# One decoder layer on one core: AdaLN's sixth part in the gate-and-up stage, and four smaller moves

## The chip, the cores and the metric

The kernel is one program on one core of a Trainium2 chip (trn2). A core has TensorE for matmuls (PE in the profile, its weight loads PEld), VectorE (DVE), ScalarE (ACT), GpSimd (POOL), and SyncE (SP), which here only issues DMAs. Each engine takes its instructions in program order from its own queue and waits on semaphores for the others. The metric is the time of one execution in microseconds (us), the median of several.

## The reference

A hybrid decoder layer, 1024 tokens wide 1024. AdaLN gives six vectors from the conditioning c; the third (gate_m) and the sixth (gate_f) multiply what the mixer and the feed-forward give.

```python
def reference(x, c, positions, w_ada, b_ada, w_in, sinks, ...):      # x 1 x 1024 x 1024, float32
    c_act = silu(c)
    mod = c_act @ w_ada + b_ada                                      # 6 parts of 1024
    shift_m, scale_m, gate_m, shift_f, scale_f, gate_f = split(mod, 6)
    u = x * (1 + scale_m) + shift_m
    y = mixer(u, ...)          # qkv and two gates from w_in; windowed attention with sinks (16 heads,
                               # 2 kv heads) -> ya; dilated attention (24 heads) -> yb;
                               # (sigmoid(ga) * ya + sigmoid(gb) * yb) @ w_o
    x = layer_norm(ALPHA * x + (1 + gate_m) * y, ln1_g, ln1_b)
    u = x * (1 + scale_f) + shift_f
    y = (silu(u @ w_gate) * (u @ w_up)) @ w_down                     # D_FF = 2816
    return layer_norm(ALPHA * x + (1 + gate_f) * y, ln2_g, ln2_b)
```

## The kernel before

All products are done in two halves of float32: a factor is split into a rounded high part (ScalarE copies it to float32r, `w_hi`) and the rest (VectorE subtracts, `w_lo`), and TensorE does three matmuls hi·hi, hi·lo, lo·hi for each pair of tiles (`mac`). Weights come through the class `Weights` (`ws`): `send` lets SyncE load 128x512 pieces into three buffers `w_raw` ahead of use, `scale` multiplies a piece by a gate on GpSimd where it needs one, `step` splits it. The engines' order is the order of the code (`manual_schedule`): a wait in an engine's queue holds everything behind it.

The stages, in order of time:

1. **Opening.** `c` is loaded and `c_act` = silu(c) worked out on ScalarE and VectorE; `ones` (128x128) is filled by VectorE. `keep_warm(8)` has TensorE multiply `ones` by itself eight times, then two matmuls with `ones` spread `c_act` over all partitions (`pt`, copied to `c_all` by ScalarE), then `keep_warm(21)` fills the time until VectorE has summed the first two AdaLN parts (`ada_sum`), ScalarE has made the first `u`, and the first real matmul (L377) can go.
2. **Projections and attention.** 46 column blocks of w_in, attention for 12 + 8 units, rotary on GpSimd. At the end two gate columns (`tail_gates`) are projected, turned into sigmoids by ScalarE in the tile `r`, and stored to `ga_d`; the last of the two is stored by a DMA from ScalarE's queue.
3. **Border, then gate pairs.** The remaining 12 gate columns are done in pairs by Strassen-Winograd products (`gw`, class `Pairs`): seven products `b11 b21 t2 t1 t3 b22 t4` for eight blocks. The first eight products (n = 0 to 7) use plain weights that `piece()` splits from `w_raw`; their sums of `u` (t2, t1, t3, t4) are read back from DRAM into tiles `xs` (`load_sums`) and split by `next_sums`, one each product. `gw.load` fetches raw weights of a pair, `gw.add` makes their sums on GpSimd.
4. **Branches.** 24 steps (b = 0, 1, 2; dc = 0 to 7), each 24 matmuls and one weight piece; `o_part` splits attention outputs for them. Beside the work of stages 3 and 4 the generator `ada_steps` makes the AdaLN parts 2, 3, 4 and 5: for each part eight row blocks of w_ada (512 KB) are loaded to `a_raw` (two buffers), VectorE adds each, weighted by a value of `c_act`, into `acc` (L993, L995), and TensorE sums `acc` over partitions, by L1008 for the gates (parts 2 and 5) and by L1015 for parts 3 and 4, which go to `shsc`. One call of `next(ada)` is one row block; in steps with b = 0 it is called twice, later once.
5. **w_o.** The merged tiles are multiplied by w_o, whose pieces GpSimd has scaled by gate 2.
6. **Gate and up.** 22 pairs p of columns of w_gate_up, again by seven products (five for p = 0 to 3), `gu.split` made two products ahead (`g_prepare`); GpSimd scales the normalized rows (`gain`) in p = 3 to 10. Results go to DRAM (`h_d`).
7. **w_down and the second layer norm.** w_down's pieces are scaled by gate 5 on GpSimd.

SyncE's DMAs and ScalarE's share eight semaphores in turn; each DMA waits for the one that held its semaphore before.

Of the kernel before, what the change touches and what calls it, by code (L numbers as in the profile page):

```python
# [10 lines left out]
F32 = mybir.dt.float32  # L11
# [7 lines left out]
P = 128  # L19
# [130 lines left out]
def decoder_layer(ctx: ExitStack, tc: tile.TileContext, I, out, dbg=None):  # L150
# [14 lines left out]
    ones = const.tile([P, P], F32, name="ones")  # L165
    nc.vector.memset(ones, 1.0)
# [46 lines left out]
    for x, _ in gate_pairs[:EARLY_PAIRS]:  # L213
        add_chunk(I["w_in"][46 + x], 2, 4)
    for b, dc in steps:
        add_chunk(branch_w[b][dc], 1, 4)
# [15 lines left out]
    ws.limit = len(ws.jobs)  # L232
# [36 lines left out]
    with tc.tile_pool(name="pro", bufs=2) as pro:  # L269
        wa_t, xt_t, raw_t, early_w, mod_t, low_t = {}, {}, {}, {}, {}, {}  # L270
# [532 lines left out]
    def stream():  # L803
# [16 lines left out]
        for dc in tail_gates:  # L820
            g = att.tile([P, T], F32, name="r", bufs=1)
            last = dc == tail_gates[-1]
            sigmoid = act_sigmoid if last else sigmoid_half
            yield from project(46 + dc, lambda t, ps: sigmoid(g[:, t * TH:(t + 1) * TH], ps))
            (nc.scalar if last else nc.sync).dma_start(ga_d[dc], g)
# [155 lines left out]
    ones_r = mix.tile([P, P], F32R, name="ones_r", bufs=1)  # L981
    nc.vector.tensor_copy(ones_r, ones)

    def ada_steps():
        for m in (2, 3, 4, 5):
# [12 lines left out]
            if m in (2, 5):  # L998
                gt = (mix if m == 2 else misc).tile([P, T], F32, name=f"gate{m}", bufs=1)
# [73 lines left out]
    gw.load(0)  # L1073
    load_sums(gp, "xs", 2)
    for step in range(4):
        gw.add(0, step)
# [35 lines left out]
    for n in range(2 * EARLY_PAIRS):  # L1112
# [6 lines left out]
        next_sums(1)  # L1119
        if n == 1:  # L1120
            load_sums(mix, "o_raw", 2)
            gw.load(1)
# [32 lines left out]
    for p in range(len(gate_pairs)):  # L1155
        ps = dict(zip("ab", acc[p])) if p in acc else {}
        g, last = {}, p == len(gate_pairs) - 1
        for i in range(7):
# [16 lines left out]
            if last:  # L1175
                if i == 0:
                    send_parts(2)
                if 2 <= i < 6:
                    parts.append(o_part(bigu))
                if i >= 4:  # L1180
                    ws.step()
            elif p and i in (1, 2, 4, 6) or (p == 1 and i == 3):
                next(ada, None)
# [35 lines left out]
    for i, (b, dc) in enumerate(steps):  # L1219
# [10 lines left out]
        if i == len(steps) - 2:  # L1230
            for x in range(2):
                ws.scale(len(ws.done) + x)
# [10 lines left out]
        for _ in range(2 if b == 0 else 1):  # L1243
            next(ada, None)
# [235 lines left out]

    hs, h_raw = {}, {}
# [10 lines left out]
    for p in range(NF):  # L1492
# [11 lines left out]
        for i in range(7):  # L1504
# [56 lines left out]
            if p == 3 and i == 0:  # L1561
                gb1 = norm_params(1)
            if i == 6 and 3 <= p < 3 + NB:
# [117 lines left out]
```

## Time and profile before

| what | value |
|---|---|
| time, median of 3 runs | 1819.81 us (1819.7 to 1819.91) |
| the profiled execution's own time | 1820.77 us |
| its span, first to last instruction | 1819.0 us |
| PE busy | 1790.4 us (98%) |
| DVE, ACT, POOL busy | 1139.6, 809.9, 621.5 us |
| mean granted TensorE clock | 0.995 |

The page sums each engine's busy time over the span and follows the chain that ended last; the waits view lists who stood still for whom. What stands between 1790.4 us and the span is TensorE's idle time. In the timeline view a row has start (us from the span's start), duration, engine, line, operation, tiles, and in brackets the idle time just before it with what ended it. SPq, ACTq and POOLq are DMA issues.

### The profile page before, as it was taken

How to read it: one execution, taken by the hardware profiler on the slowest of the kernel's cores; microseconds unless marked ns; L12 is line 12 of the kernel's file. 1: busy time of each engine (PE TensorE's matmuls, PEld its weight loads, DVE VectorE, ACT ScalarE, POOL GpSimd, SP SyncE). 2: the span in 40 equal slices, each digit the busy share in tenths (PEclk: the TensorE clock that was granted, in tenths of full speed). 3: DMA queues.
4: the chain of work that ended last, by engine and by line, in shares of the span. 5: the costliest groups of instructions: out<-in, count | busy, mean ns of one | idle time of the engine just before them, and what ended most of it. 6: DMA issues, size and time to landing. Idle time of an engine off the chain costs nothing.

```text
span 1819.0 us, 24567 instructions
## 1 busy us (share of the span) xinstructions
PE 1790.4 (98%) x8906; PEld 1473.9 (81%) x8906; DVE 1139.6 (63%) x2051; ACT 809.9 (45%) x1720; POOL 621.5 (34%) x400
## 2 busy tenths in 40 slices
PE   9999999999999999999979999999999999999998
PEld 7888888888888888878768888888888888888886
DVE  7755566566657766568646965766555444764557
ACT  6654444445444777664522233743333333421122
POOL 0232233233333232125203663156664333532223
PEclk9999999999999999999989999999999999999999
DMA  9322233233233332267466633042222222442222
GB/s 360 96 74 82 83 89 105 85 86 105 83 83 97 84 101 70 83 238 248 158 209 242 208 121 129 12 151 82 81 82 81 94 82 87 151 140 80 92 77 93
DMA packets 93081, 213.83 MB, mean 118 GB/s; under 512 B 15072, under 2 KB 24864, under 8 KB 92960
## 3 DMA queue, kind: packets, MB, share of 16 engines
q1 hardware_dynamic: 92352, 210.61, 35.3%
q8 instruction: 70, 1.15, 0.3%
q0 software_dynamic: 320, 1.06, 0.1%
q10 hardware_dynamic: 288, 0.59, 0.1%
q14 instruction: 51, 0.42, 0.1%
HBM read 163.62 MB, written 34.96 MB: 109 GB/s over the span
## 4 chain that ended last, share of the span: by engine, by line
PE 87%; DVE 5%; DMA 3%; ACT 2%; issue 1%; POOL 1%; SPq 0%; DVEq 0%; POOLq 0%; ACTq 0%
PE pf L1040 23%; PE pj L191 9%; PE pj L193 8%; PE pj L192 8%; PE pf L191 5%; PE pf L192 5%; PE pf L193 5%; PE p L1040 5%; PE s L624 4%; PE po L685 3%; PE pt L662 3%; PE p L191 2%; PE p L193 2%; PE p L192 2%; DMA a_raw<-in_w_ada 1%
## 5 line engine op out<-in xcount | busy, mean ns | idle before, releaser
L191 PE MATMUL pj<-u,w_hi 128*128 128x512 f32 x736 | 302.8, 411 | 0.0
L193 PE MATMUL pj<-u,w_lo 128*128 128x512 f32 x736 | 288.9, 392 | 0.0
L192 PE MATMUL pj<-u,w_hi 128*128 128x512 f32 x736 | 288.3, 392 | 0.0
L551 POOL TENSOR_TENSOR rb<-rb,sin_t 128x512 f32<-128x512 f32 x64 | 85.6, 1338 | 517.0 <-DVE rb L549 466.6
L145 DVE TENSOR_TENSOR w_lo<-r,w_hi 128x512 fp32r<-128x512 f32 x128 | 132.5, 1038 | 137.2 <-ACT w_hi L144 136.7
L191 PEld LDWEIGHTS pj<-u,w_hi 128*128 128x128 f32 x736 | 138.7, 188 | 31.6 <-issue 5.8
L79 DVE TENSOR_TENSOR w_lo<-w_raw,w_hi 128x512 fp32r<-128x512 f32 x132 | 121.0, 920 | 67.9 <-ACT w_hi L78 67.4
L193 PEld LDWEIGHTS pj<-u,w_lo 128*128 128x128 f32 x736 | 138.2, 188 | 30.6
L640 ACT ACTIVATE probs<-probs,st 128x128 f32<-128x128 f32 (+1 forms) x320 | 145.6, 461 | 31.0 <-DVE st L629 30.7
L192 PEld LDWEIGHTS pj<-u,w_hi 128*128 128x128 f32 x736 | 138.9, 189 | 22.3
L192 PE MATMUL pf<-wd,h 128*128 128x512 f32 x352 | 137.1, 389 | 0.0
L193 PE MATMUL pf<-wd,h 128*128 128x512 f32 x352 | 137.1, 389 | 0.0
L191 PE MATMUL pf<-wd,h 128*128 128x512 f32 x352 | 137.1, 389 | 0.0
L62 POOL TENSOR_TENSOR w_raw<-w_raw,gate 128x512 f32<-128x512 f32 x60 | 86.9, 1465 | 144.4 <-DMA w_raw<-in_w_down 117.8
L1594 DVE SCALAR_TENSOR_TENSOR zt<-zt,pf 128x512 f32<-128x512 f32 x112 | 75.2, 684 | 78.9 <-PE pf L193 78.8
L78 ACT ACTIVATE w_hi<-w_raw 128x512 fp32r<-128x512 f32 x132 | 81.7, 622 | 86.9 <-PE p L192 48.8
L552 POOL TENSOR_TENSOR r<-ra,rb 128x512 f32<-128x512 f32 x63 | 116.2, 1845 | 4.9
L664 ACT ACTIVATE ptsb<-pt 128x512 f32<-128x512 f32 (+1 forms) x128 | 63.5, 548 | 99.3 <-PE pt L662 99.0
L565 ACT ACTIVATE qs<-r 64x1024 fp32r<-64x1024 f32 x38 | 40.2, 1059 | 101.4 <-POOL r L552 100.9
L566 DVE TENSOR_TENSOR qs<-r,qs 64x1024 fp32r<-64x1024 f32 x38 | 46.4, 1220 | 57.2 <-ACT qs L565 56.5
L624 PE MATMUL s<-kh,qs 128*128 128x256 f32 (+1 forms) x320 | 79.8, 283 | 2.4 <-DVE st L629 1.7
L624 PE MATMUL s<-kl,qs 128*128 128x256 f32 (+1 forms) x320 | 80.1, 280 | 0.0
(382 smaller groups left out, 4407.5 us busy)
## 6 DMA issues: line engine op xcount, KB each, us to landing
w_raw<-in_w_in SPq DMA_DIRECT2D x100, 256.0 KB
r<-in_w_gate_up SPq DMA_DIRECT2D x44, 512.0 KB
a_raw<-in_w_ada SPq DMA_DIRECT2D x32, 512.0 KB
w_raw<-in_w_down SPq DMA_DIRECT2D x44, 256.0 KB
h_raw<-h_d SPq DMA_DIRECT2D x22, 512.0 KB
h_d<-g SPq DMA_DIRECT2D x39, 256.0 KB
wa<-in_w_ada_m SPq DMA_DIRECT2D x16, 512.0 KB
gt<-ga_d SPq DMA_DIRECT2D x16, 512.0 KB
```

The lines of the kernel that those rows point to most:

```text
L62: self.nc.gpsimd.tensor_tensor(self.raws[i], self.raws[i], scale(), op=OP.mult)
L78: self.nc.scalar.activation(hi, raw, AF.Copy)
L79: self.nc.vector.tensor_tensor(lo, raw, hi, op=OP.subtract)
L145: self.nc.vector.tensor_tensor(lo, src, hi, op=OP.subtract)
L191: nc.tensor.matmul(ps, w[0], m[0], start=first, stop=False)
L192: nc.tensor.matmul(ps, w[0], m[1], start=False, stop=False)
L193: nc.tensor.matmul(ps, w[1], m[0], start=False, stop=last)
L551: eng.tensor_tensor(b, b, sin_t[:, s], op=OP.mult)
L552: eng.tensor_tensor(residue_half(res, r, t), by_residue(a, r), by_residue(b, r), op=OP.add)
L624: nc.tensor.matmul(pss[h][:, i, lo:], box["q"][h][:, b * P:(b + 1) * P], ks[h][:, (b - 1 + lo) * P:(b + 1) * P], start=i == 0 and n == 0, ...
L640: nc.scalar.activation(pr, pr, AF.Exp, scale=-1.0, bias=st[:, 0, h, b:b + 1], accum_out=st[:, 1, h, b:b + 1])
L1040: nc.tensor.matmul(ps, w[:, c], m[:, k], start=first and k == 0 and n == 0, stop=k == 3 and n == 2, skip_group_check=True)
```

## The change

- `ones` is now a float32r tile `ones_r`, seen as float32 through a bitcast; it is filled by a memset of a temporary `one` and a copy, both placed at the start of the pool `pro`, and the later tile `ones_r` of the branch stage goes.
- The last gate of the projection stage uses tile `vt` in place of `r`, and its store is issued by GpSimd.
- At the border, `gw.load(0)` and its sums come after product 0, the loads of the sums two after products 1 and 2 each, `gw.load(1)` after product 4. The first three pieces of w_branch are sent in the last gate pair (`ws.limit`), no longer at the border.
- `ada_steps` makes parts 2, 3 and 4 only, with one call in each branch step. A new generator `last_ada` makes part 5 in the gate-and-up stage: a load after product 3 and an addition after product 6 of each pair from p = 2, then split, bias load, sum on TensorE.
- In the last five branch steps pieces of w_o that are on their way are scaled at once.

```diff
--- before.py
+++ after.py
@@ -162,8 +162,8 @@
     b_pp = const.tile([P, 48], F32, name="b_pp")
     ident = const.tile([P, P], F32, name="ident")
     nc.scalar.dma_start(ident, I["k_ident"])
-    ones = const.tile([P, P], F32, name="ones")
-    nc.vector.memset(ones, 1.0)
+    ones_r = const.tile([P, P], F32R, name="ones")
+    ones = ones_r.bitcast(F32)
 
     def split(hi, lo, src):
         nc.scalar.activation(hi, src, AF.Copy)
@@ -212,6 +212,7 @@
     EARLY_PAIRS = 4
     for x, _ in gate_pairs[:EARLY_PAIRS]:
         add_chunk(I["w_in"][46 + x], 2, 4)
+    ws.limit = len(ws.jobs)
     for b, dc in steps:
         add_chunk(branch_w[b][dc], 1, 4)
     late, wd_t, pools = {}, {}, {"bigu": bigu}
@@ -229,7 +230,7 @@
         for kp in range(4):
             add_chunk(I["w_o"][eh, kp], 2, 1, lambda eh=eh: gates[2][:, eh * 512:(eh + 1) * 512],
                       pair_dest(late, kp, lambda kp: "low", "o_hl") if eh else None)
-    ws.limit = len(ws.jobs)
+    branches_end = len(ws.jobs)
     groups = [2, 3, 4, 3, 3, 3, 4]
     down_pool = lambda f: "low" if sum(f >= e for e in np.cumsum(groups)) % 2 else "bigu"
     for f in range(NF):
@@ -267,6 +268,9 @@
     early_src = [*range(EARLY), 46 + early_gate_dc]
     NE = len(early_src)
     with tc.tile_pool(name="pro", bufs=2) as pro:
+        one = pro.tile([P, P], F32, name="one", bufs=1)
+        nc.vector.memset(one, 1.0)
+        nc.vector.tensor_copy(ones_r, one)
         wa_t, xt_t, raw_t, early_w, mod_t, low_t = {}, {}, {}, {}, {}, {}
 
         def fetch(j):
@@ -818,11 +822,11 @@
                 yield from project(46 + lead_gate_dc, lambda t, ps: act_sigmoid(g[:, t * TH:(t + 1) * TH], ps))
                 nc.sync.dma_start(ga_d[lead_gate_dc], g)
         for dc in tail_gates:
-            g = att.tile([P, T], F32, name="r", bufs=1)
             last = dc == tail_gates[-1]
+            g = att.tile([P, T], F32, name="vt" if last else "r", bufs=1)
             sigmoid = act_sigmoid if last else sigmoid_half
             yield from project(46 + dc, lambda t, ps: sigmoid(g[:, t * TH:(t + 1) * TH], ps))
-            (nc.scalar if last else nc.sync).dma_start(ga_d[dc], g)
+            (nc.gpsimd if last else nc.sync).dma_start(ga_d[dc], g)
 
     lengths = [8 if n == 0 else 24 if "b" in un else 24 if un["a"] == 0 else 8 for n, un in enumerate(units)]
     ends = np.cumsum(lengths)
@@ -978,11 +982,8 @@
 
     shsc = misc.tile([P, 2, KC], F32, name="shsc")
 
-    ones_r = mix.tile([P, P], F32R, name="ones_r", bufs=1)
-    nc.vector.tensor_copy(ones_r, ones)
-
     def ada_steps():
-        for m in (2, 3, 4, 5):
+        for m in (2, 3, 4):
             acc = mix.tile([P, T], F32, name="acc", bufs=1)
             raws = {}
             for k in range(KC + 1):
@@ -995,8 +996,8 @@
                     nc.vector.scalar_tensor_tensor(acc, raws[k - 1], c_act[:, k - 1:k], acc, op0=OP.mult, op1=OP.add)
                 yield
             yield
-            if m in (2, 5):
-                gt = (mix if m == 2 else misc).tile([P, T], F32, name=f"gate{m}", bufs=1)
+            if m == 2:
+                gt = mix.tile([P, T], F32, name="gate2", bufs=1)
                 nc.sync.dma_start(gt, I["b_ada"][:, m * D:(m + 1) * D].to_broadcast([P, D]))
                 hl = [mix.tile([P, T], F32R, name="a_hl", tag="a_raw", bufs=2) for _ in range(2)]
                 split(*hl, acc)
@@ -1070,10 +1071,6 @@
 
     load_sums(mix, "o_raw", 2)
     load_sums(mix, "a_raw", 2)
-    gw.load(0)
-    load_sums(gp, "xs", 2)
-    for step in range(4):
-        gw.add(0, step)
     acc, gated = {}, {}
     done, stored = [], []
 
@@ -1117,8 +1114,15 @@
             piece()
         prepare(n + 4 - 2 * EARLY_PAIRS)
         next_sums(1)
+        if n == 0:
+            gw.load(0)
+            for step in range(4):
+                gw.add(0, step)
         if n == 1:
+            load_sums(gp, "xs", 2)
+        if n == 2:
             load_sums(mix, "o_raw", 2)
+        if n == 4:
             gw.load(1)
         after()
         if n in (4, 6, 7):
@@ -1175,6 +1179,8 @@
             if last:
                 if i == 0:
                     send_parts(2)
+                    ws.limit = branches_end
+                    ws.send()
                 if 2 <= i < 6:
                     parts.append(o_part(bigu))
                 if i >= 4:
@@ -1227,9 +1233,9 @@
             mac(ps[t], w(k), (parts[k][:, 0, s], parts[k][:, 1, s]), k == 0, k == 3)
             if n == 3:
                 ws.step()
-        if i == len(steps) - 2:
-            for x in range(2):
-                ws.scale(len(ws.done) + x)
+        if i >= len(steps) - 5:
+            for j in range(len(ws.done), ws.sent - 1):
+                ws.scale(j)
         if i == len(steps) - 1:
             ws.step()
         if (b == 0 and 2 <= dc < 6) or (b == 1 and dc in (3, 5)):
@@ -1240,8 +1246,7 @@
             parts, following = following, []
         for t in range(2):
             merge(b, dc, t, ps[t], gts.get(i))
-        for _ in range(2 if b == 0 else 1):
-            next(ada, None)
+        next(ada, None)
         fetch_gate(i + 1)
         if i == 2 * KC + 1:
             mg, _ = wide("m", bigu)
@@ -1478,6 +1483,32 @@
             prepared[0] += 1
 
 
+    def last_ada():
+        acc5 = misc.tile([P, T], F32, name="gate5", bufs=1)
+        for k in range(KC):
+            raw = ev.tile([P, T], F32, name="a_raw", bufs=1)
+            nc.sync.dma_start(raw, I["w_ada"][k * P:(k + 1) * P, 5 * D:])
+            yield
+            if k == 0:
+                nc.vector.tensor_scalar(acc5, raw, c_act[:, 0:1], None, op0=OP.mult)
+            else:
+                nc.vector.scalar_tensor_tensor(acc5, raw, c_act[:, k:k + 1], acc5, op0=OP.mult, op1=OP.add)
+            yield
+        hl = [ev.tile([P, T], F32R, name=n, tag=n, bufs=1) for n in ("a_raw", "a_lo")]
+        split(*hl, acc5)
+        yield
+        nc.sync.dma_start(acc5, I["b_ada"][:, 5 * D:].to_broadcast([P, D]))
+        yield
+        for t in range(2):
+            s = slice(t * TH, (t + 1) * TH)
+            ps = ps_x.tile([P, TH], F32, name="px")
+            for x in range(2):
+                nc.tensor.matmul(ps, ones_r, hl[x][:, s], start=x == 0, stop=x == 1)
+            nc.vector.tensor_tensor(acc5[:, s], ps, acc5[:, s], op=OP.add)
+        nc.vector.tensor_scalar(acc5, acc5, 1.0, None, op0=OP.add)
+        gates[5] = acc5
+
+    ada = last_ada()
     hs, h_raw = {}, {}
 
     def h_load(f):
@@ -1560,6 +1591,8 @@
                     ws.step()
             if p == 3 and i == 0:
                 gb1 = norm_params(1)
+            if p > 1 and i in (3, 6):
+                next(ada, None)
             if i == 6 and 3 <= p < 3 + NB:
                 gain(p - 3, gb1)
     gb2 = norm_params(2)
```

The order of instructions shows three places. First VectorE's queue at the very start (`ones`, `one`: the 128x128 tiles of ones; `wa`: AdaLN weights). Before:

```order
L166 MEMSET ones 128x128
L175 TENSOR_SCALAR c_act<-c_act 128x8
L176 RECIPROCAL c_act<-c_act 128x8
L177 TENSOR_TENSOR c_act<-c_act,c_raw 128x8
L309 TENSOR_TENSOR diag<-ident,c_act 128x512 x2
L328 TENSOR_SCALAR b_pp<-b_pp 128x8
```

Now:

```order
L175 TENSOR_SCALAR c_act<-c_act 128x8
L176 RECIPROCAL c_act<-c_act 128x8
L177 TENSOR_TENSOR c_act<-c_act,c_raw 128x8
L272 MEMSET one 128x128
L273 CAST ones<-one 128x128
L313 TENSOR_TENSOR diag<-ident,c_act 128x512 x2
```

The filling of `ones` has moved behind the three instructions on `c_act`, and a copy has been added.

Second, SyncE's queue at the border between projection and gate pairs. Before:

```order
L55 DMA w_raw<-in_w_in 128x512
L728 DMA wb<-wa_d 64x1024 x2
L1058 DMA xs<-t_d 128x2x512 x4
L112 DMA r_7655<-in_w_in 128x1024
L112 DMA r_7656<-in_w_in 128x1024
L1058 DMA xs<-t_d 128x2x512 x2
L55 DMA w_raw<-in_w_in 128x512 x3
L1058 DMA xs<-t_d 128x2x512 x2
L112 DMA r_7721<-in_w_in 128x1024
L112 DMA r_7722<-in_w_in 128x1024
L55 DMA w_raw<-in_w_branch_a 128x512 x3
```

Now:

```order
L55 DMA w_raw<-in_w_in 128x512
L732 DMA wb<-wa_d 64x1024 x2
L1059 DMA xs<-t_d 128x2x512 x4
L55 DMA w_raw<-in_w_in 128x512 x2
L112 DMA r_7682<-in_w_in 128x1024
L112 DMA r_7683<-in_w_in 128x1024
L55 DMA w_raw<-in_w_in 128x512
L1059 DMA xs<-t_d 128x2x512 x4
L112 DMA r_7778<-in_w_in 128x1024
L112 DMA r_7779<-in_w_in 128x1024
```

Two of the weight pieces have moved ahead of the raw weights of the first pair, the third ahead of the sums of t3 and t4; the branch pieces are no longer here.

Third, VectorE's queue in the gate-and-up stage, from product 6 of one pair to product 1 of the next (`g`: the two halves of h; `c`: a kept product; `s`: the sums whose splits are the weights of t2 and t1). Before:

```order
L145 TENSOR_TENSOR w_lo<-r_11123,w_hi 128x512
L1536 TENSOR_TENSOR g<-g,pf 128x512
L1537 TENSOR_TENSOR g<-g,c_11264 128x512
L145 TENSOR_TENSOR w_lo<-s_11225,w_hi 128x512
L145 TENSOR_TENSOR w_lo<-s_11224,w_hi 128x512
L1530 TENSOR_TENSOR g<-g,pf 128x512
```

Now:

```order
L1567 TENSOR_TENSOR g<-g,pf 128x512
L1568 TENSOR_TENSOR g<-g,c_11233 128x512
L1495 SCALAR_TENSOR_TENSOR gate_10956<-a_raw,c_act,gate_10956 128x1024
L145 TENSOR_TENSOR w_lo<-s_11192,w_hi 128x512
L145 TENSOR_TENSOR w_lo<-s_11191,w_hi 128x512
L1561 TENSOR_TENSOR g<-g,pf 128x512
```

One addition of 128x1024 stands between the second product of the gate (L1568) and the split for t2.

## The prediction

> **What bounds the kernel now.** The page comes first: it says which engine has no room.
>
> ```profile
> PE 1790.4 (98%) x8906; PEld 1473.9 (81%) x8906; DVE 1139.6 (63%) x2051; ACT 809.9 (45%) x1720; POOL 621.5 (34%) x400
> ```
>
> TensorE is the bound. The change adds no matmul and takes none away, so it can gain at most what TensorE idles or runs slowly, and it loses wherever a new wait reaches TensorE. The waits view lists who keeps TensorE (total us, times, longest):
>
> ```profile
> PE p L1015 <- DVE acc L995: 11.2, 1, 11.2
> PE p L1040 <- DVE w_lo L79: 2.9, 2, 2.0
> PE p L1008 <- DVE a_hl L170: 1.4, 1, 1.4
> PE po L317 <- DVE ones L166: 1.1, 1, 1.1
> PE p L191 <- DVE gy L1208: 1.0, 1, 1.0
> PE pj L363 <- ACT u L348: 0.3, 1, 0.3
> ```
>
> Four of the six are touched: L1015 (part 3 of AdaLN), L1040 (the border), L191 (w_o), and L317 (the opening). The table of stages then shows where there is no idle time to hide anything in:
>
> ```profile
> 1200.00:1400.00 200.00, 200.00 (x884) 165.65 (x884) 115.38 (x116) 78.23 (x140) 120.21 (x72) 1.00 0.27 92
> ```
>
> In gate and up TensorE is busy 200 of 200 us; VectorE (115) has room on average, but only the moment counts.
>
> **The long wait goes.** The timeline of TensorE around it, and around its twin for part 4 (the same eight small matmuls without a wait):
>
> ```profile
> 928.00 0.39 PE L193 MATMUL p<-o_hl,w_lo 128*128 128x512 f32 x1
> 939.60 3.54 PE L1015 MATMUL p<-ones,acc 128*128 128x1 f32 x16 [11.21 <-DVE acc L995]
> 943.00 0.78 PE L191 MATMUL p<-o_hl,w_hi 128*128 128x512 f32 x1
> ...
> 946.02 0.39 PE L192 MATMUL p<-o_hl,w_hi 128*128 128x512 f32 x1
> ...
> 976.87 0.39 PE L193 MATMUL p<-o_hl,w_lo 128*128 128x512 f32 x1
> ...
> 978.90 0.48 PE L191 MATMUL p<-o_hl,w_hi 128*128 128x512 f32 x1
> ...
> 980.59 0.39 PE L192 MATMUL p<-o_hl,w_hi 128*128 128x512 f32 x1
> ```
>
> From the last ordinary matmul to the first one after L1015 it is 15.00 us (928.00 to 943.00) against 2.03 for the twin (976.87 to 978.90): 12.97 lost. Then the clock is still down: the next seven starts take 3.02 us (to 946.02) against 1.69 (978.90 to 980.59), 1.33 more. Together **14.3 us**, more than the 11.2 of the waits view. Why `acc` is late:
>
> ```profile
> 913.04 1.32 SPq L991 DMA_DIRECT2D a_raw<-in_w_ada  x2
> 922.51 1.28 DVE L995 SCALAR_TENSOR_TENSOR acc<-a_raw,c_act,acc 128x1024 f32<-128x1024 f32 x1 [10.55 <-DMA a_raw<-in_w_ada]
> ```
>
> Each branch step with b = 0 asks for two row blocks (1 MB) beside its weights, and a block issued at 913.04 is there at 922.5, 9.5 us later. The step lasts 5.44 us (24 matmuls, 0.227 apart). With one call per step, the matmul of part 3 moves from the end of step 3 (928.2) to the end of step 7, 928.2 + 4 x 5.44 = 950.0. Even if each of the blocks 3 to 7 took 9.5 us and two were in flight, the chain from 913.0 goes 922.5, 924.4, 933.5, 935, 944.3 and the last addition ends at 945.6: 4.4 us in hand. Taken: the whole 14.3; bounds 0 and 14.3. VectorE stands still on blocks meanwhile, but a step's weight piece is split before its addition and needed three steps later, so TensorE does not feel it. Part 4 follows at the end of step 17 and is used only after w_o.
>
> **The border.** The waits of 2.05 and 0.90 us:
>
> ```profile
> 799.21 0.50 PE L1040 MATMUL p<-u,w_lo 128*128 128x512 f32 x1 [2.05 <-DVE w_lo L79]
> 799.55 0.63 PE L1040 MATMUL p<-u,w_hi 128*128 128x512 f32 x2
> 785.59 9.49 SPq L1058 DMA_DIRECT2D xs<-t_d  x2
> SPq L1058 <- DMA ga_d<-r: 8.7, 1, 8.7
> 794.71 1.06 ACT L1029 ACTIVATE t2h<-xs 128x1024 fp32r<-128x1024 f32 x1 [6.39 <-DMA ga_d<-r]
> 800.25 0.63 ACT L78 ACTIVATE w_hi<-w_raw 128x512 fp32r<-128x512 f32 x1 [3.01 <-DMA w_raw<-in_w_in]
> ```
>
> One store is behind both: `ga_d<-r`, issued by ScalarE. ScalarE's copy to t2h waits 6.39 us for it (with the next weight split queued behind), and SyncE's next load waits 8.7 us for it because the store holds the semaphore whose turn it is; the three weight pieces queued behind it are issued only after 795.1 (785.59 + 9.49). With the store on GpSimd's queue and from `vt`, SyncE's turn and t2h are free of it, and two pieces go out ahead of the first pair's weights. Each wait also costs 0.11 for the refill (0.34 from 799.21 to 799.55, otherwise 0.23). Gain **3.2 us**, bounds 0 and 3.2. Late next, at worst: the raw weights of pair 0, now issued only when the second piece's buffer is free, and needed as sums at the ninth product, eight products of 12 matmuls (2.7 us each) after the first.
>
> **w_o.** TensorE waits 0.96 for a bank that `gy` frees:
>
> ```profile
> 1056.07 0.39 PE L191 MATMUL p<-w_hi,m 128*128 128x512 f32 x1
> 1053.04 0.63 ACT L78 ACTIVATE w_hi<-w_raw 128x512 fp32r<-128x512 f32 x1 [5.51 <-POOL w_raw L62]
> 1058.23 2.38 DVE L79 TENSOR_TENSOR w_lo<-w_raw,w_hi 128x512 fp32r<-128x512 f32 x2
> 1060.54 1.27 DVE L1208 TENSOR_TENSOR gy<-p,gt 128x512 f32<-128x512 f32 x2
> ```
>
> The last branch step, whose banks `gy` empties, ended where w_o begins, at 1056.07; VectorE came 4 us late, held by two splits of pieces that GpSimd had scaled late. Scaled sooner, and with part 5 gone from VectorE here, `gy` comes 2 to 3 us sooner. Gain **1.1 us** (0.96 and a refill), bounds 0 and 1.1. The 1.4 of L1008 (part 2) stays: its order is unchanged.
>
> **The opening, a cost.** TensorE's first work waits for `ones`:
>
> ```profile
> 0.84 0.17 DVE L166 MEMSET ones<- 128x128 f32 x1 [0.84 <-PEq L1670]
> 3.54 0.17 DVE L177 TENSOR_TENSOR c_act<-c_act,c_raw 128x8 f32<-128x8 f32 x1
> 786.57 0.21 DVE L982 CAST ones_r<-ones 128x128 fp32r<-128x128 f32 x1
> 4.63 3.18 PE L321 MATMUL pt<-diag,ones 128*128 128x512 f32 x4
> 7.65 4.85 PE L317 MATMUL po<-ones 128*128 128x128 f32 x42
> 10.89 0.63 ACT L348 ACTIVATE u<-ut 128x512 fp32r<-128x512 f32 x1
> 18.44 1.02 PE L363 MATMUL pj<-u,e_hi 128*128 128x512 f32 x2 [0.34 <-ACT u L348]
> ```
>
> `ones` was ready at 1.01. In the new order the memset stands behind L177, which ends at 3.71 because it waits for `c`; with memset and copy (0.17 and 0.21) `ones` is ready at 4.09: 3.1 us later. TensorE then runs eight warming products, L321, 21 more, and the first real matmul at 12.25 without a gap, while `u` was ready at 11.52. All of that, `u` included (it hangs on L321), moves by 3.1. Only the wait of 0.34 at 18.44, set by a load, swallows some. After it TensorE has no idle time until the attention, so **+2.8 us** stays; bounds 0 (the loads set the pace) and 3.1.
>
> The rows above show the rate full again at 946.02, 6.4 us after work resumed at 939.60. [...]
>
> **Gate and up, a cost.** An addition of 128x1024 now stands in front of the split for t2:
>
> ```profile
> 1305.87 2.75 POOL L1366 TENSOR_TENSOR zt<-zt,gb 128x1024 f32<-128x1024 f32 x1
> 1306.87 2.31 DVE L1537 TENSOR_TENSOR g<-g,c 128x512 f32<-128x512 f32 x1
> 1309.10 1.28 DVE L145 TENSOR_TENSOR w_lo<-s,w_hi 128x512 fp32r<-128x512 f32 x2
> 1310.90 0.39 PE L1040 MATMUL pf<-t2h,w_lo 128*128 128x512 f32 x1
> 1381.97 0.68 DVE L1537 TENSOR_TENSOR g<-g,c 128x512 f32<-128x512 f32 x1
> L995 DVE SCALAR_TENSOR_TENSOR acc<-a_raw,c_act,acc x28: 1272/1284/2312, 833.0 to 1026.5; 128x1024 f32<-128x1024 f32 x28
> ```
>
> The split for t2 ends at 1309.78 and its weight load starts 0.23 before 1310.90, at 1310.67: 0.9 us in hand. The addition takes 1.28 (median), so the split ends at about 1310.98. By the border's rows the matmul starts 0.05 after, the next 0.34 later, at 1311.37 in place of 1311.13: 0.24 us lost. This place comes once a pair; eight additions are made (p = 2 to 9), but p = 2's feeds a pair without the first two products and is a short first one. So 7 x 0.24 = **1.7 us**. Bounds: 0 if VectorE comes earlier, and 8.9 if each addition takes the longest of the 28, 2.31 (1.03 more, 7 x 1.27). Taken near the low end: the GpSimd work that doubles L1537 (2.31 against 0.68 without it) ends at 1308.62, before the addition starts. The rest of part 5 costs nothing: its four matmuls (0.9) leave the branch stage and come back here, the splits for p = 10 and the last sums on VectorE have 2 us and more in hand, and each load has a whole pair (19 us) to land.
>
> **The sum.** -14.3 - 3.2 - 1.1 + 2.8 + 1.7 = -14.1. The profiled execution took 1820.77 (span 1819.0 and 1.77 around it): span 1804.9, time 1806.7. The median of the runs is 0.96 below that execution, so the forecast for the median is **1805.7 us**.
>
> **Rivals.** (1) *The new costs are hidden* (0.15): the opening is paced by loads and the split for t2 slips through: -18.6, 1801.2. The 0.34 at 18.44 speaks for it, the gapless TensorE from 12.25 on against. (2) *The additions run into GpSimd* (0.13): 8.9 in place of 1.7, 1812.9. It needs GpSimd's gain 0.5 us later than it is. [...] (3) *The long wait only moves* (0.05): a block takes over 10.5 us to land and TensorE waits at step 7 as it did at step 3: 14.3 back, 1820.0, no change. The widest landing seen, 9.5, speaks against it. (4) *The border still waits*, now for the store on GpSimd's queue or the later raw weights (0.05): 1808.9. (5) *Slower* (0.04): in gate and up a row block lands after VectorE wants it. VectorE then holds the split for t2 and TensorE stands, eight times. A block's buffer is free when the addition before it ends (1310.4 in the rows above), and the next addition comes a pair later (84 matmuls, 19.0 us, after 1309.1): 17.7 us. At 21 us of landing 3.3 are lost eight times, 26 us, and the time is 1832; past the 1823.4 of a measurable loss it gets at 19.9 us. Against it: this stage's DMA share of 0.27 at 92 GB/s, to which the blocks add 27.
>
> **How the numbers follow.** The forecast holds 0.58. A measurement of this kernel tells 0.2% (3.6 us) from no change: 1816.2 and below is faster. Forecast and rivals 1, 2 and 4 are (0.91); rival 3 is no change (0.05); rival 5 slower (0.04). The range 1801.5 to 1811.5 takes the forecast with the bounds of the opening, the border and w_o, most of rival 1, and rival 2 up to additions of about 2.1 us.
>
> **What would show it.** Right: no L1015 wait in the waits view and a granted clock of 1.00 from 900 to 950; no L1040 wait at the border; TensorE's first matmul at about 4.2 and the first real one at about 15.4; seven short waits of TensorE for `w_lo` in gate and up, 0.1 to 0.3 each. Wrong: a wait on `acc` or `a_raw` at step 7, a first real matmul at 12.3, or waits over 1 us in gate and up.

## The result

The changed kernel takes **1805.86 us** (median of six, 1804.71 to 1806.85) against 1819.69 us (median of six, 1817.68 to 1819.91) of the kernel before on the same chip: ratio 0.9926, 95% interval 0.9913 to 0.9939, or 13.8 us less. The forecast was 1805.7. The profiled execution took 1804.71 us with a span of 1802.9.

### The profile after

The first line of the page's first part (busy time, share and instructions of each engine), then the waits view of TensorE (total us, times, longest):

```profile
PE 1786.3 (99%) x8906; PEld 1469.5 (82%) x8906; DVE 1147.7 (64%) x2051; ACT 810.3 (45%) x1720; POOL 619.2 (34%) x401
```

```profile
PE po L321 <- DVE ones L273: 4.1, 1, 4.1
PE s L628 <- DVE st L633: 1.7, 6, 0.3
PE p L1009 <- DVE a_hl L170: 1.4, 1, 1.4
PE pf L191 <- DVE zt L1325: 0.9, 1, 0.9
PE pf L1041 <- DVE spare L1450: 0.3, 1, 0.3
```

The 11.2 for `acc`, the 2.9 for `w_lo` at the border and the 1.0 for `gy` are gone. The wait for `ones` is longer, as expected; that for `zt` (0.26 before) and the one for `spare` were not in the forecast. The 1.4 for `a_hl` stays. The seven waits in gate and up do not show here, since the weight load waits in TensorE's place; they stand in the waits view of the weight loads and, for one pair, in the timelines of VectorE and of the weight loads:

```profile
PEld pf L1041 <- DVE w_lo L145: 2.7, 7, 0.4
```

```profile
1291.21 1.27 DVE L1495 SCALAR_TENSOR_TENSOR gate<-a_raw,c_act,gate 128x1024 f32<-128x1024 f32 x1
1292.41 1.28 DVE L145 TENSOR_TENSOR w_lo<-s,w_hi 128x512 fp32r<-128x512 f32 x2
1293.14 0.19 PEld L1041 LDWEIGHTS pf<-t2h,w_lo 128*128 128x128 f32 x1 [0.38 <-DVE w_lo L145]
```

The addition ends, the split starts, and the weight load comes 0.38 after it was due. The place of the long wait now, in TensorE's timeline and in the table of stages (busy time of PE, PEld, DVE, ACT, POOL with counts, granted clock, DMA share, GB/s):

```profile
946.54 0.39 PE L193 MATMUL p<-o_hl,w_lo 128*128 128x512 f32 x1
946.77 1.84 PE L1016 MATMUL p<-ones,acc 128*128 128x1 f32 x16
948.47 0.49 PE L191 MATMUL p<-o_hl,w_hi 128*128 128x512 f32 x1
```

```profile
900.00:950.00 50.00, 50.00 (x231) 41.66 (x230) 24.99 (x30) 22.14 (x36) 0.03 (x1) 1.00 0.70 228
```

Part 3 is summed at 946.77 without a wait and TensorE is busy for all 50 us at clock 1.00. The last addition into `acc` stands on VectorE like this, so 9.3 us were in hand (937.43 to 946.77):

```profile
936.15 1.28 DVE L996 SCALAR_TENSOR_TENSOR acc<-a_raw,c_act,acc 128x1024 f32<-128x1024 f32 x1
```

The opening, TensorE:

```profile
4.12 3.46 PE L321 MATMUL po<-ones 128*128 128x128 f32 x16 [4.12 <-DVE ones L273]
7.41 1.88 PE L325 MATMUL pt<-diag,ones 128*128 128x512 f32 x4
9.13 4.85 PE L321 MATMUL po<-ones 128*128 128x128 f32 x42
13.74 0.48 PE L381 MATMUL pj<-u,e_hi 128*128 128x512 f32 x1
```

TensorE starts 3.06 later than before, but its first real matmul (L381) comes only 1.49 later: the four matmuls on `diag` took 1.88 in place of 3.18. The trace's own record of the clock explains it: the rate rose from half to full at 7.09, 3.0 us after TensorE's start, so all four ran fast; before, it rose at 7.21, 6.2 us after the start, and three of the four ran slowly.

### Where the time went

The same matmul looked up in both timelines, at the ends of the stages. The last column is the step from one row to the next.

| matmul | before | after | difference | step |
|---|---|---|---|---|
| first real one | 12.25 | 13.74 | +1.49 | +1.49 |
| behind the load wait of the opening | 19.29 | 20.40 | +1.11 | -0.38 |
| end of the attention | 779.08 | 779.62 | +0.54 | -0.57 |
| end of the plain products, after the border | 889.69 | 886.48 | -3.21 | -3.75 |
| first of w_o | 1056.07 | 1037.50 | -18.57 | -15.36 |
| w_o, behind the place of `gy` | 1061.27 | 1041.58 | -19.69 | -1.12 |
| second half of w_o | 1101.27 | 1082.04 | -19.23 | +0.46 |
| opening of gate and up | 1171.59 | 1152.67 | -18.92 | +0.31 |
| t2 of the pair after the last addition | 1349.21 | 1332.08 | -17.13 | +1.79 |
| t3, after part 5's matmuls | 1373.01 | 1356.85 | -16.16 | +0.97 |
| last matmul | 1810.70 | 1794.57 | -16.13 | +0.03 |

The step of -15.36 holds the four matmuls of part 5, which come back later as the +0.97; the long wait alone is 14.39. The total, 16.1, is larger than the 13.8 between the medians: the profiled execution of before (1820.77) was slower than its median and had the longest ramp of the clock seen in the opening, that of the change was the fastest of its six and had the shortest. The two ramps differ by 1.57 (12.25 - 1.06 = 11.19 against 13.74 - 4.12 = 9.62), which is no effect of the change, as the runs below show.

### The profile page after: what moved, and what is told of

It is laid out like the page before. It is cut to its first block, busy times and chain, and to the rows that moved or that the text cites. A ratio compares the mean times of both kernels' runs of the same rounds, so it can differ in the third digit from the quotient of the medians.

```text
span 1802.9 us, 24555 instructions
## 1 busy us (share of the span) xinstructions
PE 1786.3 (99%) x8906; PEld 1469.5 (82%) x8906; DVE 1147.7 (64%) x2051; ACT 810.3 (45%) x1720; POOL 619.2 (34%) x401
## 4 chain that ended last, share of the span: by engine, by line
PE 94%; DVE 3%; ACT 2%; issue 1%; POOL 0%; DMA 0%; DVEq 0%; ACTq 0%
PE pf L1041 23%; PE pj L191 9%; PE pj L193 9%; PE pj L192 8%; PE p L1041 6%; PE pf L191 5%; PE pf L193 5%; PE pf L192 5%; PE s L628 4%; PE p L191 3%; PE p L193 3%; PE p L192 3%; PE po L689 3%; PE pt L666 3%; DVE qs L570 1%; ACT probs L644 1%
## 5 line engine op out<-in xcount | busy, mean ns | idle before, releaser
L145 DVE TENSOR_TENSOR w_lo<-r,w_hi 128x512 fp32r<-128x512 f32 x128 | 140.2, 1099 | 118.7 <-ACT w_hi L144 118.3
L79 DVE TENSOR_TENSOR w_lo<-w_raw,w_hi 128x512 fp32r<-128x512 f32 x132 | 124.8, 949 | 81.3 <-ACT w_hi L78 80.8
L126 POOL TENSOR_TENSOR s<-r 128x512 f32<-128x512 f32 x27 | 36.1, 1336 | 128.1 <-DVE w_lo L145 96.4
```

The costliest lines, as they stand in the source:

```text
L79: self.nc.vector.tensor_tensor(lo, raw, hi, op=OP.subtract)
L145: self.nc.vector.tensor_tensor(lo, src, hi, op=OP.subtract)
```

## The experiments

All edits are on the changed kernel. "Control" is the changed kernel itself, run again beside the runs that move the ones and the additions and beside the first faster version. The runs with two calls, with halves of the border undone and with the scaling undone were made on another chip; a later series of the changed kernel there (the second control below) gave 1805.52 in place of 1806.70, so a difference of about 1 us between the medians of these runs and the control proves nothing, and the timelines decide.

### The changed kernel again, and the opening

> The changed kernel again, unaltered, as the measure for the runs beside it. Two readings of the result stand against each other. (a) The sum of the prediction was right as it stands (-14.1): this execution again lies 13 to 15 us below the kernel before in the median, and its opening may show a ramp of the clock of another length than the 3.3 us that the first profile showed (the kernel before: 6.1), because the ramp varies from one execution to the next. (b) The short ramp belongs to the later start: the profile shows 3.3 us of half rate again, within 0.3, and the first real matmul again at 13.7 within 0.3.

Measured: **1806.70** (1806.06 to 1807.5), ratio to before 0.9925 (0.9912 to 0.9939). From first matmul (3.92) to first real one (14.49) it took 10.57, not 9.62; the clock rose 4.9 us after the first matmul, not 3.0. Reading (a) holds: the short ramp was chance.

Now the tile of ones is filled first again:

```diff
+    with tc.tile_pool(name="first", bufs=1) as first:
+        one = first.tile([P, P], F32, name="one")
+        nc.vector.memset(one, 1.0)
+        nc.vector.tensor_copy(ones_r, one)
     c_act = const.tile([P, KC], F32, name="c_act")
...
-        one = pro.tile([P, P], F32, name="one", bufs=1)
-        nc.vector.memset(one, 1.0)
-        nc.vector.tensor_copy(ones_r, one)
```

> The tile of ones is filled at the head of VectorE's queue again, the rest as changed. The prediction's term (+2.8, the opening shifts everything) expects 2.8 us less than the control, first matmul at about 1.3, first real one 2.8 or more before the control's. The rival, that later waits swallow the shift (the wait of 0.34 for u at 18.4 and that of 0.6 for qs in the attention, which come back here), expects 0.4 to 1.1 us less than the control. A third, that the opening is set by loads altogether, expects no difference, within 0.3.

Measured: **1804.89** (1804.49 to 1805.36), 1.8 below the control; ratio to before 0.9915 (0.9902 to 0.9929). TensorE's timeline and two rows of the waits view:

```profile
1.32 3.78 PE L323 MATMUL po<-ones 128*128 128x128 f32 x16 [1.32 <-DVE ones L176]
...
11.94 0.48 PE L383 MATMUL pj<-u,e_hi 128*128 128x512 f32 x1
...
18.32 1.02 PE L369 MATMUL pj<-u,e_hi 128*128 128x512 f32 x2 [0.54 <-ACT u L354]
```

```profile
PE s L630 <- DVE qs L572: 0.6, 1, 0.6
```

The ramp was the control's (10.62 against 10.57), so the two timelines can be compared: the first real matmul comes 2.55 earlier, 1.98 are left behind the wait for `u`, 1.6 at the end of the attention, 1.9 at 900 and 2.2 at the end of the program. The opening passes on some 2 us, between the prediction's 2.8 and the 0.4 to 1.1 of the rival reading. What swallows the rest is as the rival said, the waits for `u` (0.54) and `qs` (0.6 against 0.2).

### One call or two per branch step

```diff
-        next(ada, None)
+        for _ in range(2 if b == 0 else 1):
+            next(ada, None)
```

> Branch steps with b = 0 ask for two row blocks again, as before; the rest as changed. The prediction's account of the long wait (the matmul of part 3 stands at the end of step 3 while the blocks land 9.5 us after their issue) expects the wait of TensorE for acc back, 10 to 12 us, with the clock at half rate for some 3 us after it: 14.3 us above the control of 1806.7, about 1821. The rival, that the wait belonged to the crowd of loads at that time, which part six, the border loads and the pieces sent sooner have changed, expects a much smaller wait, 0 to 6 us, and 1807 to 1813.

Measured: **1820.89** (1817.87 to 1827.45, nine), 14.2 above the control (15.4 above the second one, on the same chip) and no faster than before (ratio 1.001, 0.9998 to 1.0023). Waits view and TensorE's timeline:

```profile
PE p L1016 <- DVE acc L996: 8.9, 1, 8.9
PE pf L191 <- DVE zt L1326: 1.8, 1, 1.8
```

```profile
925.88 0.39 PE L193 MATMUL p<-o_hl,w_lo 128*128 128x512 f32 x1
935.13 3.54 PE L1016 MATMUL p<-ones,acc 128*128 128x1 f32 x16 [8.85 <-DVE acc L996]
938.53 0.77 PE L191 MATMUL p<-o_hl,w_hi 128*128 128x512 f32 x1
```

One line brings the long wait back with its half rate (0.77 for the next matmul), although part 5 is out of the branch stage and the border is as changed. The number of calls is the cause. That moving part 5 is what allows one call is argued, not tried: part 4 came ten steps behind part 3 (1003.02 and 946.77), and a third part would end behind the last of the 24 steps. In the profiled execution the loss in the branch steps is 12.4, and 1.0 more is the wait for `zt`; the wait itself is 2.4 shorter than before, so the crowd of loads had a small share. The spread of its nine times is about 10 us. The two longest had the lowest granted clock (1827.45 at 0.992, 1824.52 at 0.993, the shortest 1817.87 at 0.995), so part of the spread is time at half rate; the rest is open.

### The border, undone by halves

The store back on ScalarE's queue and in tile `r`, the new order of loads kept:

```diff
-            g = att.tile([P, T], F32, name="vt" if last else "r", bufs=1)
+            g = att.tile([P, T], F32, name="r", bufs=1)
...
-            (nc.gpsimd if last else nc.sync).dma_start(ga_d[dc], g)
+            (nc.scalar if last else nc.sync).dma_start(ga_d[dc], g)
```

> The last gate is stored by ScalarE from the tile r again; the new order of the border loads stays. If the store is behind both border waits, as predicted, ScalarE's copy to t2h waits 5 us or more for it again, and a load of SyncE's waits 5 us or more for its semaphore; TensorE waits for w_lo 1 to 3 us at the border: 1 to 3.2 us above the control of 1806.7. If it was the order of the loads that took the waits away, TensorE waits 0.3 or less there and the time is the control's within 0.3.

Measured: **1808.43** (1806.78 to 1809.23), 1.7 above the control (2.9 above the second); ratio to before 0.9937 (0.9922 to 0.9952). ScalarE's timeline, SyncE's waits and TensorE's waits:

```profile
795.68 1.06 ACT L1030 ACTIVATE t2h<-xs 128x1024 fp32r<-128x1024 f32 x1 [5.37 <-DMA ga_d<-r]
```

```profile
SPq L112 <- DMA ga_d<-r: 2.9, 1, 2.9
```

```profile
PE p L1041 <- ACT sx L1145: 1.3, 1, 1.3
PE p L1041 <- DVE w_lo L145: 0.6, 2, 0.4
PE p L1041 <- ACT gt L1142: 0.2, 1, 0.2
```

The store holds ScalarE 5.37 again, but no plain product waits: the pieces ahead in SyncE's queue were there. ScalarE and VectorE fall behind by the splits of the sums, and TensorE pays 15 us later, at 810 to 820, for `w_lo` of the first pairs, `gt` and `sx`. From the end of the attention to 890 the execution loses 2.8 against the control's.

The old order, with the store as changed:

```diff
     load_sums(mix, "a_raw", 2)
+    gw.load(0)
+    load_sums(gp, "xs", 2)
+    for step in range(4):
+        gw.add(0, step)
...
-        if n == 0:
-            gw.load(0)
-            for step in range(4):
-                gw.add(0, step)
         if n == 1:
-            load_sums(gp, "xs", 2)
-        if n == 2:
             load_sums(mix, "o_raw", 2)
-        if n == 4:
             gw.load(1)
...
-    ws.limit = len(ws.jobs)
     for b, dc in steps:
         add_chunk(branch_w[b][dc], 1, 4)
...
-    branches_end = len(ws.jobs)
+    ws.limit = len(ws.jobs)
...
-                    ws.limit = branches_end
-                    ws.send()
```

> The border loads go out in the old order again (the raw weights of the first pair ahead of the plain pieces, the branch pieces at the border); the store stays on GpSimd's queue and in the tile vt. If the store alone was behind the waits, the border has no wait over 0.5 and the time is the control's 1806.7 within 0.5. If the order carries them, TensorE waits 2 to 3 us for w_lo at the border: about 1809.5.

Measured: **1807.97** (1807.33 to 1809.52), 1.3 above the control (2.5 above the second); ratio 0.9937 (0.9922 to 0.9952). TensorE's waits and ScalarE's timeline:

```profile
PE p L1040 <- ACT w_hi L78: 0.8, 1, 0.8
```

```profile
801.34 0.63 ACT L78 ACTIVATE w_hi<-w_raw 128x512 fp32r<-128x512 f32 x1 [9.36 <-DMA w_raw<-in_w_in]
```

The store is out of the way (the copies to t2h wait for nothing), yet the pieces queued behind 1 MB of raw weights and two sums land late by themselves: 9.36 us of ScalarE, 0.84 of TensorE. From the end of the attention to 890 this execution loses 1.2 against the control's. The halves, 2.8 and 1.2, come to 4.0; the whole step was 3.75 in the two timelines above, and 3.2 in those of both controls.

### Scaling sooner, undone

```diff
-        if i >= len(steps) - 5:
-            for j in range(len(ws.done), ws.sent - 1):
-                ws.scale(j)
+        if i == len(steps) - 2:
+            for x in range(2):
+                ws.scale(len(ws.done) + x)
```

> Pieces of w_o are scaled in the last step but one again, two of them, as before; the rest as changed. The prediction's term for w_o expects the wait for gy of about 1.0 back and 1.1 us more than the control of 1806.7. The rival, that taking part 5 from VectorE's queue there was enough, expects no such wait and the control's time within 0.3.

Measured: **1806.03** (1805.36 to 1806.38), 0.7 below the control, 0.5 above the second, and so within the spread of such runs; ratio 0.9925 (0.991 to 0.9939). The view of TensorE's waits has no row for `gy`; the longest row of the second half of the program is

```profile
PE pf L191 <- DVE zt L1325: 1.1, 1, 1.1
```

So scaling sooner gains nothing on its own. What took the wait away is then, by the rows, part 5's leaving VectorE's queue: in the kernel before, its last two instructions (L1009, L1010) hold VectorE from 1042.02 to 1044.60, ahead of the last three `gy`, and the last starts 4.5 us behind the first matmul of w_o; here it starts 2.5 behind, with the sooner scaling 1.5. No run puts part 5 back alone.

### The additions in another place

```diff
-            if p > 1 and i in (3, 6):
+            if (p > 1 and i == 5) or (p > 2 and i == 4):
                 next(ada, None)
```

> The additions of part 5 are made after product 4 of each pair from p = 3 on, in front of a split that has 2 us in hand, and the loads after product 5; the rest as changed. The prediction's term for gate and up (7 x 0.24 = 1.7) expects the seven waits of the weight loads for w_lo (0.38 each) to be gone and the time 1.7 to 1.8 us below the control. The rival, that an addition anywhere in VectorE's queue costs TensorE as much (it only moves), expects waits of the same size at another product and no difference, within 0.3.

Measured: **1805.68** (1805.43 to 1807.12), 1.0 below the control; ratio 0.9922 (0.991 to 0.9935). The row of seven waits is gone from the weight loads, and one new wait stands in TensorE's timeline:

```profile
1348.81 0.50 PE L1041 MATMUL pf<-b21h,w_lo 128*128 128x512 f32 x1 [1.40 <-DVE w_lo L145]
```

Up to 1334 the timelines show 0.25 to 0.3 gained at each pair, the prediction's price; then the split of part 5 (128x1024, on ScalarE and VectorE), which this edit moved too, to after product 5 of pair 10, takes 1.4 and a refill back. By the timelines the edit nets 0.3; the rest of the 1.0 is a shorter ramp in the opening. The rival, that an addition costs as much anywhere, falls.

### Towards a faster version

The first had ones first, the additions moved as above, one more `yield` between the split of part 2 and its matmul, and two PSUM tiles allocated and not used ahead of w_o's eight:

```diff
                 split(*hl, acc)
                 yield
+                yield
...
+    for _ in range(2):
+        ps_2.tile([P, TH], F32, name="p2")
     banks = [ps_2.tile([P, TH], F32, name="p2") for _ in range(NB)]
```

> Ones first, additions after product 4, one more step between the split of part 2 and its matmul (the wait of 1.4 for a_hl, with its refill 1.5), and two PSUM banks of w_o passed over in turn, so that the first product of the second half of w_o gets the bank that it had before (wait for zt 0.26 in place of 0.85). By the prediction's terms: -2.8 - 1.8 - 1.5 - 0.6 = 6.7 us below the control; if later waits swallow the opening, 4.3 to 5.0 below it. Against that stands that a wait taken away comes back at the next place, as a wait for another tile: then 2 us or less below the control.

Measured: **1803.21** (1802.56 to 1805.73), 3.5 below the control; ratio 0.9909 (0.9895 to 0.9922). The wait for `a_hl` is gone and the 1.40 above is there; the wait for `zt` has grown to 1.56. The unused tiles moved nothing. VectorE's timelines show what the wait hangs on. The additions that empty the eight PSUM banks of w_o's first half (`zt`) run in the order of the row blocks 0 to 7, and the waiting matmul starts 0.15 us behind the end of one of them: of block 4 in the kernel before, of block 5 in the changed one, and of block 6 in this one and in the one with two calls. That is the block whose bank the second half takes first. The matmul that waits, in the kernel before, the changed one, this one and the one with two calls:

```profile
1101.27 0.47 PE L191 MATMUL pf<-o_hl,m 128*128 128x512 f32 x1 [0.26 <-DVE zt L1320]
```

```profile
1082.04 0.47 PE L191 MATMUL pf<-o_hl,m 128*128 128x512 f32 x1 [0.85 <-DVE zt L1325]
```

```profile
1080.37 0.47 PE L196 MATMUL pf<-o_hl,m 128*128 128x512 f32 x1 [1.56 <-DVE zt L1328]
```

```profile
1096.51 0.47 PE L191 MATMUL pf<-o_hl,m 128*128 128x512 f32 x1 [1.82 <-DVE zt L1326]
```

Next, part 5's split went to product 3 of pair 11 and two of w_o's tiles were exchanged:

```diff
+            if (2 <= p <= 9 and i == 5) or (3 <= p <= 10 and i == 4) or (p, i) in ((11, 3), (11, 5), (12, 3)):
                 next(ada, None)
...
+    banks[3], banks[6] = banks[6], banks[3]
```

> The changed kernel once more, for the run beside it: 1806.7 within 0.7; from TensorE's first matmul to its first real one 9.6 to 11.2 us, the spread that nine executions of these kernels have shown.

> Ones first; additions after product 4, the split of part 5 after product 3 of pair 11 in place of product 5 of pair 10; one more step between the split of part 2 and its matmul; and two banks of w_o exchanged, so that the bank that the second half of w_o takes first (bank 0) is that of the fourth row block, not of a late one. By the waits seen: opening -1.8, additions -1.8, a_hl -1.5, zt -0.9: 6.0 us below the control, about 1800.7, with no wait for zt and none of 1.4 for w_lo in gate and up. If the bank of the second half of w_o is not what sets the wait for zt, that wait stays at 0.8 to 1.6 and the time is 1801.6 or more.

Measured: control **1805.52** (1805.13 to 1806.14), lower than was expected, this **1801.96** (1801.65 to 1803.03), 3.6 less; ratio to before 0.9908 (0.9894 to 0.9923). The 1.4 for `w_lo` is gone, but `zt` waits 2.07. The exchange in the code did not help: the matmul still starts 0.15 behind the addition of block 6. So the expectation on `zt` missed through its edit, not through the mechanism. The last edit leaves the banks and changes the order in which VectorE empties them:

```diff
+    turn = [0, 1, 2, 3, 6, 4, 5, 7]
-    for tb in range(NB):
-        residual(banks[tb], tb, 0)
+    for n, tb in enumerate(turn):
+        residual(banks[tb], tb, 0)
```

(with x loaded in the same order, and without the exchange).

> As the best so far (ones first, additions after product 4, one more step for part 2), and in w_o the block whose bank the second half takes first is added and released ahead of the other three late ones (the order of the blocks on VectorE is 0 1 2 3 6 4 5 7). If the bank sets the wait for zt (before: bank of block 4, wait 0.26; changed: block 5, 0.85; later variants: block 6, 1.6 to 2.1), the wait falls to 0.5 or less and the time to 1800 to 1800.8. If the loads of x are late for any order, the wait stays above 1 and the time at 1802.

> The same without the new order of blocks, for comparison on the same chip: 1802.0 within 0.7, wait for zt 1.5 to 2.2.

Measured: **1800.42** (1799.99 to 1800.75), ratio to before **0.9891** (0.9878 to 0.9905), against 1803.15 (1801.31 to 1804.29), ratio 0.9905 (0.9892 to 0.9918), of the version without the new order on the same chip (its median is above the 1802.0 within 0.7 that was expected, its `zt` waits 1.5). The wait:

```profile
1079.86 0.47 PE L196 MATMUL pf<-o_hl,m 128*128 128x512 f32 x1 [0.19 <-DVE zt L1328]
```

The matmul again starts 0.15 behind the addition of block 6, which is now the fifth. So the bank sets this wait; of the 2.7 between the two medians it accounts for 1.3. This version beats both kernels: 19.3 us below the one before on the same chip, some 5 below the changed one as its three series showed it (1805.86, 1806.70, 1805.52).

## Why the prediction was right, and where it was not

The mechanism, the direction and the total are right, and the long wait, 14.3 of the 14.1 net, was the term that mattered. By its terms:

| term | predicted | in the two timelines | by experiment |
|---|---|---|---|
| long wait of part 3 | -14.3 | -14.39 | two calls: +14.2 |
| border | -3.2 | -3.75 (both controls -3.2) | halves: 2.8 and 1.2 by timeline, 1.7 and 1.3 by medians |
| w_o | -1.1 | -1.12 | not from the scaling |
| opening | +2.8 | +0.54, with equal ramps about +2.1 | ones first: -1.8 |
| gate and up | +1.7 | +1.79 | seven waits gone when moved |
| not foreseen | - | zt +0.46, spare +0.31 | zt: the bank |
| sum | -14.1 | -16.1, with equal ramps -14.6 | medians: -13.8 |

**The long wait.** The step count was exact: part 3 came at 946.77, and 950.0 less the 3.2 already gained is 946.8. The blocks came sooner than the bound that was worked out, so 9.3 us were in hand, and rival 3 (the wait only moves) never came near.

**Gate and up.** Price and count held: 0.26 a pair, seven times. Rival 2 did not come: the seven additions took 1.27 each, each behind the GpSimd instruction beside which L1568 took 2.30 (L1371; 0.68 at 1365.84, with no GpSimd work beside it) and which ended 0.47 us before the addition began, as the rows of before had said. Rival 5 did not come either: no addition of this stage waited for its row block.

**The border** was rightly sized and wrongly explained. "One store is behind both" failed: with the store undone alone the two waits on plain pieces stayed away, and with the order undone alone one of them came back. The store's cost is the lag of ScalarE and VectorE, the order's the lag of the pieces; in the kernel before both fell on the same matmuls and looked like one.

**w_o.** The size was right, and of the two reasons that the prediction gave together (scaled sooner, part 5 gone from VectorE) the second is enough: the wait stayed away with the scaling undone. `gy` came 2.0 sooner without the sooner scaling and 3.0 with it, as the prediction had it.

**The opening** was mis-sized: 2.8 against about 2. The step that failed rests on "After it TensorE has no idle time until the attention": that holds, but in the attention TensorE waits for `qs` (0.6 before and with ones first, 0.2 in the control), and that wait shrank, as did the one for `u` (0.34 before, none after). A delay is not passed on whole through a later wait on something that does not move with it: with ones first the gain of 2.55 was 1.98 behind the wait for `u`. That the two timelines show only 0.54 is the ramp: it was 1.57 shorter, which is also why the first real matmul came at 13.74 and not at the forecast 15.4. The prediction's sum took the ramp as in the kernel before (11.19). In the profiled execution it was shorter by 1.57; in the control, with the same late start, by 0.62. Three executions of the changed kernel took 9.62, 10.57 and 9.72 from the first matmul to the first real one: it differs from one execution to the next, and leaving it out of the sum for the median was right.

**Not foreseen.** The bank that the second half of w_o takes first is that of row block 5 in place of 4: 0.46. Which of the edits moved it was not tried; the run with two calls, where part 5 is gone too, had block 6. And in the opening of gate and up a split for `spare` (0.31) that was just in time came late; with ones first this wait is absent, and its cause was not traced.

So the closeness of 1805.7 to 1805.86 owes something to luck: in the two timelines 0.7 too much for the opening and 0.5 too little gained at the border stand against 0.8 of waits left out, and the medians moved 0.8 less than the timelines with equal ramps.

## What to carry to other kernels

When a generator is advanced once or twice per step, work out from the trace how long one of its loads takes to land and at which step its last consumer stands: here the step back to two calls, one line, took the whole gain away. In gate and up an addition of 1.27 us cost 0.26 a pair ahead of a split with 0.9 us in hand, and its seven waits were gone when it stood ahead of one with 2 us, so count the slack at the very instruction behind it. Before crediting one cause with two waits, undo the halves apart, and look whether a new wait stands further down: the store's cost came back 15 us later under other names.

## What the hardware showed that was not expected

**The clock was down for 13.66 us after two stalls of different length.** In the kernel before, the last ordinary matmul ahead of the long wait starts at 928.00, in the one with two calls at 925.88. The table of stages around the steps of the granted clock, before and with two calls (the clock is the third number from the end):

```profile
932.00:933.00 1.00, 0.00 (x0) 0.00 (x0) 1.00 (x2) 0.00 (x0) 0.00 (x0) 0.61 0.91 223
...
945.00:946.00 1.00, 1.00 (x4) 0.79 (x3) 0.09 (x1) 0.00 (x0) 0.00 (x0) 0.56 0.99 350
```

```profile
928.00:930.00 2.00, 0.00 (x0) 0.00 (x0) 0.95 (x1) 0.00 (x0) 0.00 (x0) 0.65 0.77 203
...
942.00:943.00 1.00, 1.00 (x5) 0.78 (x4) 0.53 (x1) 0.00 (x0) 0.00 (x0) 0.87 1.04 188
```

Before, the mean is 1.00 ahead of 932 and 0.50 from 933 to 945, so 0.61 over this stretch of 1 us puts the fall at 932.22; in the same way the rise is at 945.88 before, and the two steps at 928.60 and 942.26 with two calls. Fall to rise is 13.66 in both (13.65 in the trace's own record of the clock, from which the views take their means), though TensorE stood 11.2 in the one and 8.9 in the other. After the restart (939.60 and 935.13) the rate stayed at half for 6.3 and 7.1 us, so in these two the rise did not come at one distance from the restart. What sets it was not shown.

**The opening's ramp varies by 1.6 us from one execution to the next.** From TensorE's first matmul to its first real one it took 9.62 to 11.19 us in the 14 profiled executions (11.19 and 9.62 are the two kernels of the comparison). By the record of the clock the half rate lasted from 3.0 us (the changed kernel) to 6.2 us (the kernel before) after the first matmul; what sets its length was not shown. Much of the 2 us spread between runs of one kernel can come from this (an estimate: 9.62 to 11.19 alone is 1.6 of it). The views give a granted clock of 1.00 in this stretch because the record begins with the rise; there only the duration of the matmuls shows the half rate (L321 of the changed kernel: 16 in 3.46, then 42 in 4.85).
